# A list scheduler that repeats itself with ranks from latest start times

## The chip, the cores and the metric

The kernel runs on one core of a Trainium2 chip, as one program. The metric is device time in microseconds (us). It was timed three times; the median is 1887.29 us. One further execution was taken by the profiler, and every row shown here is from that one.

## The reference

One inference step of a layer with three kinds of head that read the same normalised input. 2048 prompt tokens and 8 x 16 sample tokens, model width 1024, all in float32.

```python
h = rms_norm(x, norm_g) @ w_in                 # 1024 -> 3654 columns
fox_cols, rwkv_cols, mem_cols = jnp.split(h, [FOX_COLS, FOX_COLS + RWKV_COLS], axis=-1)
q, k, v, logf, g_f = fox_prep(fox_cols, fox_q_g, fox_k_g, fox_b_f)
o_f = fox_prompt(q, k, v, logf)                # 6 heads x 64, causal softmax with a forget bias
xs = token_shift(rwkv_cols, shift_prev, rwkv_mu)
o_r, s_new, g_r = rwkv_branch(xs, rwkv_s0, ...)  # 6 heads x 64, S <- S diag(w) + S(-kk)^T(a kk) + v^T k
o_m = mem_attend(mq, mem_q_g, mk, mv)          # 4 heads x 64 against 256 memory tokens
o = jnp.concatenate([o_f * silu(g_f), o_r * silu(g_r), o_m * silu(g_m)], axis=-1)
y = x + o @ w_out
```

The sample tokens do the same with cached keys and values, and a state of their own for the recurrence. Outputs are y, the new keys, values and forget values, and the states.

## The kernel before

Large products are done as three matmuls of rounded parts: each operand is split into a high part (a copy rounded to the PE's fast 32-bit format) and a low part (the rest), and high x high, high x low and low x high are added. Small products stay plain float32.

**Projection phase.** Four blocks `it` of 512 tokens (the first with the 128 sample tokens). A block normalises its input (`prep_x`), and projects it in groups of 256 columns: `wd_load` brings a group's split weights (tiles `w`, four buffers in tag `hl`; the first time from the input through ACT and POOL, later from a copy `w_d` in DRAM), `proj_d` (`pjd`) or `wide` (`pjt`) multiplies. Results are copied out of PSUM (`qk`, `gth`, two buffers each) and stored to DRAM.

In each block three RWKV visits `p` of two heads each are made, twelve prompt visits in all, and three for the samples. A visit is a long chain of small steps. `rwkv_in` makes the decayed factors (`AR`, `bk`; `bk` has one buffer), multiplies them chunk by chunk (`gr` into `gm`), writes diagonal blocks to DRAM (`ld<-gm`, line 436), loads them the other way round (`yt<-ld`, line 438), inverts them on DVE in 28 small operations (`ytmp`, `yt`), writes them back (`ld<-yt`, line 447) and loads them into place (`xd<-ld`, eight transfers, line 451). `rwkv_mid` transposes `xd` (lines 464 and 477), joins the blocks with 32x32 matmuls (`gw`, `gx`), and turns factors with the PE (`pvt`, `pat`, `pbt`); the last of these reads `bk`. `rwkv_scan` carries the state through eight chunks, one after the other, and `rwkv_out` normalises and stores.

**Attention phase.** It begins where the buffers of the first phase end: its pools in SBUF and PSUM lie over those of the first. Twelve units (three head pairs x four query blocks) of forgetting attention: `pm` for row maxima, `pS` scores, `P` exponentials split into `Ph` and `Pl`, `po` values. Between them stand eight units against the memory, the sample units (`sA` to `sD`), and the output projection (`py`), in three parts.

**Order.** The kernel is first written out in program order. `_arrange` then re-sorts it. `_program` lists for each instruction an engine, a duration by a formula (`_Op`), what it depends on and which tiles it uses. `_visits` joins neighbouring small matmuls into one node. `_schedule` runs through the nodes as a simulated machine: it repeatedly takes, over all engines, the node that could start earliest. Among nodes of one engine with the same start the lowest rank wins. A tile's first user must wait for a free buffer of its tag, in program order of the tag's tiles (`pt` and `pj` may leave that order), and for the first phase's pools to be empty where its own pool lies over them. The rank is the place in program order, measured in time, less a weight times the length of the longest chain behind the node (`below`). On PE `stay` is taken off the rank of a node whose matmul shape is the one in use. Eight schedules are made (four weights, two values of `stay`), and the one with the shortest simulated total is kept. Its start times give the order on every engine, and each engine runs its instructions in that order. All transfers are issued from one queue, SP's, which runs in order too.

Of the kernel before, what the change touches and what calls it, by code (L numbers as in the profile page):

```python
# [51 lines left out]
def kernel(ctx: ExitStack, tc: tile.TileContext, I: dict, O: dict):  # L52
# [873 lines left out]
    with ExitStack() as p2:  # L926
# [523 lines left out]
_WARM = 3300  # L1450
_WINDOW = 3000
_STEP = 100
_WEIGHTS = (0.0, 0.15, 0.3, 0.45)
_STAY = (0, 2500)
_LOOSE = ("pt", "pj")


class _Pools:


    def __init__(self, tc):
        self.tc, self.open, self.below = tc, [], {}
# [236 lines left out]
        return s, s + (own - c.own) + c.time + (w - 1) * c.own  # L1699


def _schedule(prog, runs, over, weight, stay, loose=(), rank=None):

    ins, eng, cost, deps, tiles, tile = prog
    nodes, node = runs
    count = len(nodes)
    of = [eng[m[0]] for m in nodes]
    before = [sorted({node[j] for k in m for j in deps[k]} - {x}) for x, m in enumerate(nodes)]  # L1710
    used = [sorted({n for k in m for n in tiles[k]}) for m in nodes]
    seen = lambda a, b: (0 if a == "PE" else 15) if a == b != "SP" else _SEEN[b]
    succ, soft, need = [[] for _ in nodes], [[] for _ in nodes], [len(d) for d in before]
    pool = {n: t.mls.memorylocations[0].ant_tile_pool_name for n, t in tile.items()}
    first, queue, uses, left, free_at = {}, {}, {}, {}, {}
    for x in range(count):
        for j in before[x]:
            succ[j].append(x)
        for n in used[x]:
            uses[n] = uses.get(n, 0) + 1  # L1720
            left[pool[n]] = left.get(pool[n], 0) + 1
            if n not in first:
                first[n] = x
                queue.setdefault(tile[n].tag, []).append(n)
                free_at[tile[n].tag] = [0] * tile[n].tag_meta.bufs
            elif first[n] not in before[x]:
                soft[first[n]].append(x)
                need[x] += 1
    after = [sorted({q for n in used[x] for q in over.get(pool[n], ())}) for x in range(count)]
    pooled, below, at, own = {}, [0] * count, 0, [0] * count  # L1730

    def length(m, e):
        c = [cost[k] for k in m]
# [9 lines left out]
    spent = [length(m, e) for m, e in zip(nodes, of)]  # L1743
    gate = {}
    for x in range(count - 1, -1, -1):
        tail = 150 if of[x] == "PE" else 0
        below[x] = spent[x] + max([below[s] + seen(of[x], of[s]) + tail for s in succ[x]] +
                                  [gate.get(pool[n], 0) for n in used[x]], default=0)
        for q in after[x]:
            gate[q] = max(gate.get(q, 0), below[x])  # L1750
    for x in range(count):
        at += spent[x] if of[x] == "PE" else _STEP
        own[x] = at - weight * below[x]
    rank = rank or own
# [3 lines left out]
    released, alive, wire, base, order = {}, set(), 0, 0, []  # L1758
    cand = {e: [x for x in range(count) if not need[x] and of[x] == e] for e in free}

    def possible(x):
        r, taken = ready[x], {}
        for q in after[x]:
            if left.get(q):
                return None
            r = max(r, pooled.get(q, 0))
        for n in used[x]:
            if n not in alive:
                tag = tile[n].tag
                j = taken.get(tag, 0)  # L1770
                if len(free_at[tag]) <= j:
                    return None
                fresh = queue[tag][:j + 1]
                if n not in fresh:
                    if tag.rsplit("_", 2)[0] not in loose or len(free_at[tag]) <= j + 1:
                        return None
                r, taken[tag] = max(r, sorted(free_at[tag])[j]), j + 1
        return r

    while len(order) < count:  # L1780
        while done[base]:
            base += 1
        best = None
        for e, xs in cand.items():
            b = None
            for x in xs:
                r = possible(x) if x <= base + _WINDOW else None
                if r is None:
                    continue
                if e == "PE":  # L1790
                    c = cost[nodes[x][0]]
                    s, key = array.starts(c, r)
                    y = (key, rank[x] - stay * (c.shape == array.shape), x, e, s, r)
                else:
                    s = max(free[e], r)
                    y = (s, rank[x], x, e, s, r)
                if b is None or y < b:
                    b = y
            if b and (best is None or b[0] < best[0]):
                best = b  # L1800
        if not best:
            return math.inf, order, start
        _, _, x, e, s, r = best
        cand[e].remove(x)
        done[x] = True
        order.append(x)
        for n in used[x]:
# [24 lines left out]
        start[x] = s  # L1832
        gone = end[x] + 60
        for n in used[x]:
            uses[n] -= 1
            left[pool[n]] -= 1
            pooled[pool[n]] = max(pooled.get(pool[n], 0), gone)
            released[n] = max(released.get(n, 0), gone)
            if not uses[n]:
                free_at[tile[n].tag].append(released[n])  # L1840
        for z, t in [(z, s + 1) for z in soft[x]] + [(z, end[x] + seen(e, of[z])) for z in succ[x]]:
            ready[z] = max(ready[z], t if e != "PE" or of[z] != "PE" else s + 1)
            need[z] -= 1
            if not need[z]:
                cand[of[z]].append(z)
    return max(end), order, start


def _arrange(nc, tc, pools):

    prog = _program(nc)
    over, runs = _overlaps(pools, prog[-1]), _visits(prog)
# [120 lines left out]
```

## Time and profile before

| | |
|---|---|
| median of three timed runs | 1887.29 us (1883.79 to 1889.1) |
| the profiled execution, its own time | 1892.18 us |
| its span, first to last instruction | 1890.1 us |
| busy: PE, DVE, ACT, POOL | 94%, 50%, 46%, 42% |
| mean granted clock of PE | 0.954 |
| moved by the transfers | 301.34 MB, 159 GB/s on the mean |

The page cuts the span into 40 slices of 47 us. A digit is the busy share in tenths; `PEclk` is the clock granted to PE, in tenths of the full one.

```profile
PE   5979999899999999998999997899898999999998
DVE  6544444464444563453744543767445544386213
ACT  5424342424234323324232424687687555876452
PEclk9989999999999999998999896799999889999999
```

PE's low slices are the first, those near slices 24 and 25 (1130 to 1220 us), where the first phase ends, and one at slice 31 (1460 to 1500 us). The clock is low at the same places. ACT works much more in the second half, where the exponentials are.

### The profile page before, as it was taken

What the parts mean: (1) busy time and instruction counts of PE and PEld (TensorE: products, weight loads), DVE (VectorE), ACT (ScalarE), POOL (GpSimd) and SP (SyncE); (2) the same over time, 40 slices, a digit from 0 to 9 for tenths busy, and PEclk for the clock granted to TensorE, in tenths of its full rate; (3) what the DMA queues carried; (4) which work ended last, traced back from release to release, by engine and by line L of the source; (5) the groups of instructions that cost most, each with busy time, mean ns of one, the idle gap of its engine ahead of it and who ended that gap; (6) DMA issues with size and microseconds to landing.
All of it is one profiled execution on the core that took longest, in us unless ns stands there. A gap on an engine that the chain in (4) does not pass through costs nothing. (4 is left out here: it accounts for less than half of the span.)

```text
span 1890.1 us, 42104 instructions
## 1 busy us (share of the span) xinstructions
PE 1784.7 (94%) x16743; PEld 1426.4 (75%) x16743; DVE 949.0 (50%) x2330; ACT 874.9 (46%) x1727; POOL 788.9 (42%) x790
## 2 busy tenths in 40 slices
PE   5979999899999999998999997899898999999998
PEld 4878988688887888776788886666665666667776
DVE  6544444464444563453744543767445544386213
ACT  5424342424234323324232424687687555876452
POOL 5564342142132232121321331377485443866463
PEclk9989999999999999998999896799999889999999
DMA  7665455535436555354455344435546644254332
GB/s 245 228 227 169 153 175 182 191 123 176 163 117 207 177 167 196 109 176 163 127 164 188 103 155 123 141 126 167 188 137 209 186 139 137 67 179 145 137 114 100
DMA packets 213274, 301.34 MB, mean 159 GB/s; under 512 B 57444, under 2 KB 162454, under 8 KB 197206
## 3 DMA queue, kind: packets, MB, share of 16 engines
q1 hardware_dynamic: 213078, 298.66, 48.2%
q8 instruction: 131, 2.15, 0.5%
q14 instruction: 65, 0.53, 0.1%
HBM read 211.47 MB, written 87.12 MB: 158 GB/s over the span
## 5 line engine op out<-in xcount | busy, mean ns | idle before, releaser
L59 PE MATMUL pjd<-xk,w 128*128 128x512 f32 (+5 forms) x2280 | 526.4, 375 | 18.9 <-ACT qk L705 6.7
L59 PEld LDWEIGHTS pjd<-xk,w 128*128 128x128 f32 (+1 forms) x2280 | 385.8, 191 | 87.4 <-issue 9.5
L62 POOL TENSOR_TENSOR Pl<-P,Ph 128x512 fp32r<-128x512 f32 (+3 forms) x272 | 315.5, 1170 | 165.5 <-ACT Ph L1120 144.7
L59 PE MATMUL pjt<-w,xk 128*128 128x256 f32 x2040 | 290.3, 291 | 6.7 <-POOL w L62 4.2
L59 PEld LDWEIGHTS pjt<-w,xk 128*128 128x128 f32 x2040 | 266.2, 194 | 17.8 <-issue 5.0
L59 PE MATMUL py<-W,oh 128*128 128x512 f32 x816 | 247.1, 403 | 1.9 <-DVE rb L1162 0.9
L1117 ACT ACTIVATE P<-pS,NB 128x512 f32<-128x512 f32 x240 | 148.5, 623 | 110.9 <-PE pS L59 85.0
L59 PEld LDWEIGHTS py<-W,oh 128*128 128x128 f32 x816 | 150.9, 190 | 39.7 <-DVE rb L1162 1.4
L59 PE MATMUL pS<-Q,K 128*128 128x512 f32 (+2 forms) x480 | 160.1, 400 | 4.5 <-ACT P L1117 4.0
L59 PE MATMUL po<-Ph,vt 128*65 128x512 f32 x480 | 158.3, 381 | 0.3 <-ACT ob L1143 0.2
L1120 ACT CAST Ph<-P 128x512 fp32r<-128x512 f32 (+3 forms) x272 | 151.4, 564 | 9.2 <-PE po L59 4.0
L59 PEld LDWEIGHTS pS<-Q,K 128*128 128x128 f32 (+1 forms) x480 | 89.1, 198 | 36.6 <-ACT P L1117 16.0
L62 DVE TENSOR_TENSOR xo<-py,xo 128x512 f32<-128x512 f32 x68 | 46.8, 689 | 133.2 <-PE py L59 133.0
L1063 DVE CUSTOM_DVE_ANT_0 jk<-pm,nb,mx 128x512 bf16<-128x512 f32 (+3 forms) x144 | 93.0, 646 | 30.6 <-PE pm L59 22.8
L62 POOL TENSOR_TENSOR nr<-nr,mhalf 128x8 f32<-128x8 f32 (+2 forms) x43 | 61.5, 1431 | 97.5 <-DVE nr L68 73.0
L59 PE MATMUL pm<-K,Q 128*128 128x512 f32 (+2 forms) x240 | 96.4, 415 | 5.7 <-DVE mx L1063 4.8
L62 POOL TENSOR_TENSOR w<-wraw,w 128x1024 fp32r<-128x1024 f32 (+1 forms) x34 | 80.7, 2375 | 44.3 <-ACT w L197 43.2
L59 PE MATMUL po<-Pl,vt 128*65 128x512 f32 x240 | 91.1, 380 | 0.6 <-POOL Pl L62 0.6
L59 PEld LDWEIGHTS po<-Ph,vt 128*65 128x65 f32 x480 | 65.2, 141 | 26.6 <-issue 2.2
L705 ACT COPY qk<-pjt 128x512 f32<-128x512 f32 (+1 forms) x47 | 26.5, 563 | 113.1 <-PE pjt L59 92.0
L1063 DVE CUSTOM_DVE_ANT_0 jk<-pm,nb 128x512 bf16<-128x512 f32 (+3 forms) x96 | 61.3, 638 | 33.0 <-PE pm L59 28.3
L62 POOL TENSOR_TENSOR oh<-ot,oh 128x384 fp32r<-128x384 f32 (+2 forms) x38 | 45.2, 1191 | 57.0 <-ACT oh L1321 32.0
(392 smaller groups left out, 2942.6 us busy)
## 6 DMA issues: line engine op xcount, KB each, us to landing
w<-w_d SPq DMA_DIRECT2D x84, 1024.0 KB
w_d<-w SPq DMA_DIRECT2D x28, 1024.0 KB
y_d<-xo SPq DMA_DIRECT2D x21, 512.0 KB
wraw<-in_w_in SPq DMA_DIRECT2D x36, 256.0 KB
xo<-in_x SPq DMA_DIRECT2D x17, 512.0 KB
xo<-y_d SPq DMA_DIRECT2D x17, 512.0 KB
xt<-in_x SPq DMA_DIRECT2D x24, 256.0 KB
xraw<-in_xT SPq DMA_DIRECT2D x24, 256.0 KB
```

The costliest lines, as they stand in the source:

```text
L59: PE.matmul(out, lhsT, rhs, start=start, stop=stop, skip_group_check=True)
L62: e.tensor_tensor(out=out, in0=a, in1=b, op=op)
L705: S.copy(o_, out)
L1063: V.tensor_tensor_reduce(out=jk[:, :n], in0=pm[:, :n], in1=U["nb"][:, h, c0:c0 + n], scale=1.0, scalar=-3.0e38 if c0 == 0 else m_, op0=A_, ...
L1117: S.activation(P_[:, c0:], pS[:, c0:], AF.Exp, bias=NB[:, qb, 2 * hp + h, kt:kt + 1] if fox else 0.0)
L1120: S.copy(Ph[:, c0:], P_[:, c0:])
```

## The change

`_schedule` is split: what doesn't change between schedules goes into a class `_Problem` (dependencies, tiles, `below`), and the rank is handed in. `_Problem.emitted(weight)` is the old rank. While a schedule is made, it is noted for each node which earlier node's end freed the buffer or the pool that it took (`why`). At the end a pass backward over the schedule gives each node a latest start `late`: the latest at which every node that depends on it, or that waited for its buffer, can still start at its own latest. The order on the engines does not count in it. `_arrange` makes five schedules for each of three weights (0.3, 0.45, 0.6), all with `stay` 0; after each the ranks become 0.6 of the old ones plus 0.4 of `late`. The shortest of the fifteen is kept. Nothing before `_WEIGHTS` in the file changes, and the simulated machine, its durations and its rules stay.

```diff
-_WEIGHTS = (0.0, 0.15, 0.3, 0.45)
-_STAY = (0, 2500)
+_TRIES = ((0.3, 0), (0.45, 0), (0.6, 0))
+_AGAIN = 5
+_SHIFT = 0.4
...
+    def emitted(self, weight):
+
+        at, rank = 0, []
+        for x in range(self.count):
+            at += self.spent[x] if self.of[x] == "PE" else _STEP
+            rank.append(at - weight * self.below[x])
+        return rank
...
-            r = max(r, pooled.get(q, 0))
+            r = max(r, pooled.get(q, (0,))[0])
...
+        for q in p.after[x]:
+            if q in pooled:
+                why[x].append((pooled[q][1], pooled[q][0]))
         for n in used[x]:
             if n not in alive:
                 alive.add(n)
                 queue[tile[n].tag].remove(n)
                 free_at[tile[n].tag].sort()
-                free_at[tile[n].tag].pop(0)
+                at, by = free_at[tile[n].tag].pop(0)
+                if by >= 0:
+                    why[x].append((by, at))
...
-    return max(end), order, start
+    total = max(end)
+    late = [total - (end[x] - start[x]) for x in range(count)]
+    for x in reversed(order):
+        e = of[x]
+        for j in p.before[x]:
+            late[j] = min(late[j], late[x] - (1 if of[j] == e == "PE" else end[j] - start[j] + p.seen(of[j], e)))
+        for j, at in why[x]:
+            late[j] = min(late[j], late[x] - (at - start[j]))
+    return total, start, late
...
-    _, _, start = min((_schedule(prog, runs, over, w, stay, _LOOSE) for w in _WEIGHTS for stay in _STAY),
-                      key=lambda x: x[0])
+    found = []
+    for w, stay in _TRIES:
+        rank = p.emitted(w)
+        for _ in range(_AGAIN):
+            total, start, late = _schedule(p, rank, stay, _LOOSE)
+            rank = [(1 - _SHIFT) * a + _SHIFT * b for a, b in zip(rank, late)]
+            found.append((total, start))
+    _, start = min(found, key=lambda x: x[0])
```

More of the change, by code (lines that the diff above doesn't have):

```diff
@@ L1699, in run @@
         return s, s + (own - c.own) + c.time + (w - 1) * c.own
[L1702 to L1733, printed above, removed]
@@ new lines, with __init__, seen, length @@
+class _Problem:
+    def __init__(self, prog, runs, over):
+        self.ins, self.eng, self.cost, deps, tiles, self.tile = prog
+        self.nodes, node = runs
+        nodes, tile = self.nodes, self.tile
+        self.count = count = len(nodes)
+        self.of = of = [self.eng[m[0]] for m in nodes]
+        self.before = before = [sorted({node[j] for k in m for j in deps[k]} - {x}) for x, m in enumerate(nodes)]
+        self.used = used = [sorted({n for k in m for n in tiles[k]}) for m in nodes]
+        self.succ, self.soft, self.need = [[] for _ in nodes], [[] for _ in nodes], [len(d) for d in before]
+        self.pool = pool = {n: t.mls.memorylocations[0].ant_tile_pool_name for n, t in tile.items()}
+        self.queue, self.uses, self.left, first = {}, {}, {}, {}
+        for x in range(count):
+            for j in before[x]:
+                self.succ[j].append(x)
+            for n in used[x]:
+                self.uses[n] = self.uses.get(n, 0) + 1
+                self.left[pool[n]] = self.left.get(pool[n], 0) + 1
+                if n not in first:
+                    first[n] = x
+                    self.queue.setdefault(tile[n].tag, []).append(n)
+                elif first[n] not in before[x]:
+                    self.soft[first[n]].append(x)
+                    self.need[x] += 1
+        self.after = [sorted({q for n in used[x] for q in over.get(pool[n], ())}) for x in range(count)]
+        self.spent = [self.length([self.cost[k] for k in m], e) for m, e in zip(nodes, of)]
+        self.below, gate = [0] * count, {}
+        for x in range(count - 1, -1, -1):
+            tail = 150 if of[x] == "PE" else 0
+            self.below[x] = self.spent[x] + max([self.below[s] + self.seen(of[x], of[s]) + tail for s in self.succ[x]] +
+                                                [gate.get(pool[n], 0) for n in used[x]], default=0)
+            for q in self.after[x]:
+                gate[q] = max(gate.get(q, 0), self.below[x])
+    @staticmethod
+    def seen(a, b):
+        return (0 if a == "PE" else 15) if a == b != "SP" else _SEEN[b]
+    @staticmethod
+    def length(c, e):
@@ L1741, in length, with _schedule @@
         return c[0].own
[L1743 to L1754, printed above, removed]
+    def emitted(self, weight):
[4 more added lines that the diff above has]
+        return rank
+def _schedule(p, rank, stay, loose=()):
+    nodes, cost, of, used, tile, pool, count = p.nodes, p.cost, p.of, p.used, p.tile, p.pool, p.count
+    need, uses, left = list(p.need), dict(p.uses), dict(p.left)
+    queue = {t: list(q) for t, q in p.queue.items()}
+    free_at = {t: [(0, -1)] * tile[q[0]].tag_meta.bufs for t, q in queue.items()}
     free = dict.fromkeys(("PE", "DVE", "Activation", "Pool", "SP"), 0)
@@ L1757, in _schedule @@
     ready, end, done, start = [0] * count, [0] * count, [False] * count, [0] * count
-    released, alive, wire, base, order = {}, set(), 0, 0, []
+    released, alive, pooled, wire, base, order, why = {}, set(), {}, 0, 0, [], [[] for _ in nodes]
     cand = {e: [x for x in range(count) if not need[x] and of[x] == e] for e in free}
@@ L1776, in possible @@
                         return None
-                r, taken[tag] = max(r, sorted(free_at[tag])[j]), j + 1
+                r, taken[tag] = max(r, sorted(free_at[tag])[j][0]), j + 1
         return r
@@ L1801, in _schedule @@
         if not best:
-            return math.inf, order, start
+            return math.inf, start, start
         _, _, x, e, s, r = best
@@ L1806, in _schedule @@
         order.append(x)
+        for q in p.after[x]:
+            if q in pooled:
+                why[x].append((pooled[q][1], pooled[q][0]))
         for n in used[x]:
@@ L1836, in _schedule @@
             left[pool[n]] -= 1
-            pooled[pool[n]] = max(pooled.get(pool[n], 0), gone)
-            released[n] = max(released.get(n, 0), gone)
+            pooled[pool[n]] = max(pooled.get(pool[n], (0, x)), (gone, x))
+            released[n] = max(released.get(n, (0, x)), (gone, x))
             if not uses[n]:
                 free_at[tile[n].tag].append(released[n])
-        for z, t in [(z, s + 1) for z in soft[x]] + [(z, end[x] + seen(e, of[z])) for z in succ[x]]:
+        for z, t in [(z, s + 1) for z in p.soft[x]] + [(z, end[x] + p.seen(e, of[z])) for z in p.succ[x]]:
             ready[z] = max(ready[z], t if e != "PE" or of[z] != "PE" else s + 1)
@@ L1845, in _schedule @@
                 cand[of[z]].append(z)
-    return max(end), order, start
+    total = max(end)
[7 more added lines that the diff above has]
+    return total, start, late
 def _arrange(nc, tc, pools):
     prog = _program(nc)
-    over, runs = _overlaps(pools, prog[-1]), _visits(prog)
-    _, _, start = min((_schedule(prog, runs, over, w, stay, _LOOSE) for w in _WEIGHTS for stay in _STAY),
-                      key=lambda x: x[0])
+    runs = _visits(prog)
+    p = _Problem(prog, runs, _overlaps(pools, prog[-1]))
+    found = []
[6 more added lines that the diff above has]
+    _, start = min(found, key=lambda x: x[0])
     at = {}
```

1 line of the change is left out of this document (removed).

## The prediction

> **What bounds the kernel now.** I read the page first, for the busiest engine and the clock, then the windows, to place the loss by stage.
>
> ```profile
> PE 1784.7 (94%) x16743; PEld 1426.4 (75%) x16743; DVE 949.0 (50%) x2330; ACT 874.9 (46%) x1727; POOL 788.9 (42%) x790
> ...
> core 0: 1890.1 us, clock 0.954
> ```
>
> TensorE (PE) is busy 1784.7 of 1890.1 us, and no other engine passes half. Two things are lost on it: 1890.1 - 1784.7 = 105.4 us of idle time, and clock. The granted clock is 0.954 on the mean, so about 1784.7 x 0.046 = 82.1 us of the busy time is the price of the reduced clock (an estimate, which takes the mean clock for the busy time). Together 187.5 us. What is left, some 1703 us, is work that an order can't change.
>
> The windows say where it lies. Columns: from:to, length, then busy us (and instructions) of PE, PE's weight loads, DVE, ACT, POOL; clock; DMA share; GB/s.
>
> ```profile
> 0.00:50.00 50.00, 29.48 (x147) 23.52 (x148) 32.01 (x74) 28.32 (x62) 23.65 (x35) 0.93 0.81 255
> 104.00:150.00 46.00, 37.51 (x397) 35.72 (x396) 18.88 (x49) 13.45 (x23) 26.23 (x21) 0.85 0.74 243
> 1133.00:1182.00 49.00, 39.31 (x636) 31.42 (x634) 18.92 (x47) 23.19 (x48) 8.65 (x12) 0.64 0.40 118
> 1182.00:1230.00 48.00, 42.98 (x181) 28.79 (x181) 38.09 (x98) 30.55 (x61) 19.70 (x21) 0.80 0.44 139
> 1446.00:1504.00 58.00, 49.58 (x291) 34.55 (x290) 32.61 (x90) 27.55 (x57) 19.11 (x22) 0.82 0.63 192
> 1850.00:1890.10 40.10, 34.60 (x156) 25.73 (x154) 17.37 (x23) 8.67 (x17) 8.97 (x10) 1.00 0.24 89
> ```
>
> The loss of a window is its length less PE's busy time, plus busy time x (1 - clock). The head loses 20.5 + 2.1 = 22.6, waiting for the first inputs; the tail 5.5, the last additions and stores. I count both as fixed: 187.5 - 28.1 = 159.4 us can be reached by order. Of it the three stretches in between hold 68.9: the border between the projection phase and the attention phase (1133 to 1230) 23.8 + 13.6 = 37.5, the decode units (1446 on) 17.3, and 104 to 150 14.1. The remaining 90.5 is spread thinner over the other 1600 us.
>
> Why the border is bad: dense matmuls run out before the last RWKV visit's chain does.
>
> ```profile
> 1046.91 1.77 DVE L65 SCALAR_TENSOR_TENSOR e<-e,e 128x512 f32<-128x512 f32 x1
> ...
> 1069.90 2.34 DVE L65 SCALAR_TENSOR_TENSOR bk<-xsk,vh,e 128x512 f32<-128x512 f32 x1 [0.51 <-PE pbt L59]
> ...
> 1105.44 0.16 DVE L62 TENSOR_TENSOR ytmp<-yt 64x14 f32<-64x14 f32 x1
> ...
> 1109.34 0.21 DVE L62 TENSOR_TENSOR yt<-yt,ytmp 64x54 f32<-64x54 f32 x1
> 1110.40 0.69 DVE L65 SCALAR_TENSOR_TENSOR gth<-gth,pjd 128x512 f32<-128x512 f32 x1 [0.85 <-ACT gth L751]
> ...
> 1119.78 0.17 DVE L62 TENSOR_TENSOR yt<-yt,ytmp 64x14 f32<-64x14 f32 x1
> ...
> 1133.14 0.48 PE L59 MATMUL pjd<-xk,w 128*128 128x512 f32 x1
> ```
>
> These are rows of the timeline, DVE's and at the end PE's: start, length, engine, what is written from what. The last projection matmul starts at 1133.14. The visit's triangular solver (`yt`, `ytmp`) ends only at 1119.95, its result comes back from DRAM (`xd`) after 1130, and everything behind that (gw, gx, the scan, the output) runs with almost nothing dense beside it, at a clock of 0.64.
>
> **The change, part by part.** The program's instructions stay, so no count and no duration changes; what changes is the order on each engine and on SP's transfer queue. Before, the best of eight list schedules is kept (four weights, with and without a bonus for staying in a matmul shape). After, the best of fifteen: three weights without the bonus, five passes each, every next pass with ranks moved 0.4 towards the latest start that data and buffers leave in the pass before. Each pass still starts what can start earliest; the rank decides only between instructions that could start at the same time. So nothing is held back on purpose, and the gain is limited to places where something urgent stood behind something that could wait. I look for such places on the worst chain.
>
> The solver of the last visit goes from 1105.44 to 1119.95, 14.5 us. Its first 18 of 28 operations take 4.11 us to 1109.55, so 28 alone would take 4.11 / 18 x 28 = 6.4. The other 8.1 us DVE spent on instructions of gates (`gth`, at 1110.40) and norms that came between. The solver's transfers stand in SP's queue like this:
>
> ```profile
> 434.65 0.47 SPq L447 DMA_DIRECT2D ld<-yt  x1
> 436.61 3.46 SPq L451 DMA_DIRECT2D xd<-ld  x7
> ...
> 1034.72 0.46 SPq L447 DMA_DIRECT2D ld<-yt  x1
> 1040.40 0.33 SPq L192 DMA_DIRECT2D w<-w_d  x1
> 1040.82 5.04 SPq L451 DMA_DIRECT2D xd<-ld  x8
> ...
> 1120.30 0.45 SPq L447 DMA_DIRECT2D ld<-yt  x1
> ...
> 1125.79 0.46 SPq L713 DMA_DIRECT2D out_mv_p<-qk  x1
> 1126.34 3.80 SPq L451 DMA_DIRECT2D xd<-ld  x8
> ```
>
> From the write `ld<-yt` to the first `xd<-ld` an early visit needs 436.61 - 434.65 = 1.96 us; the last one 6.04 (stores of memory keys and values stand between, the last of them at 1125.79) and the one before it 6.10 (behind a weight load, `w<-w_d`). That is 4.1 us too much in each. Sum of what better ranks could take out ahead of the naked stretch: 8.1 + 4.1 + 4.1 = 16.3 us. A us less of naked chain is a us of it moved beside dense work, and the naked window (1133 to 1182) loses 23.8 / 49 = 0.49 per us. So the border yields 16.3 x 0.49 = **7.9 us**, 21% of its loss. Its bounds: 0, if these waits merely change place, and 37.5.
>
> For the other two stretches (31.4 us) I have no such count; I give them the same 21%, **6.6 us**, with 0 and 31.4 as bounds. For the thin rest I take a tenth, **9.1 us**, because a new order also makes new gaps there; its lower bound is the slower rival below, its upper one 90.5.
>
> What is moved past what: with late ranks, weight loads and the RWKV visit's transfers come ahead of result stores in SP's queue. What then becomes late are stores, and the buffers that they hold. The first row shows the kind already, the second is used below:
>
> ```profile
> PE pjd L59 <- ACT qk L705: 6.7, 2, 3.9
> ...
> PEld L59 <- issue: 24.2, 104, 0.5
> ```
>
> PE waited 6.7 us in two waits for `qk` copies, whose two buffers are free again only when their stores are through. The latest starts go through buffer releases too, so such a store gets an early date where a tile waits for its buffer. I put no net cost on it. The shape bonus goes: a change of shape shows as "issue" before weight loads, 24.2 us in 104 waits, 0.23 each, and mostly beside a busy PE. Between none and 50 changes more that is 0 to 11.5 us; I take 0, since nearly all of it is covered by the matmul before, and keep 11.5 in the range.
>
> Sum: 7.9 + 6.6 + 9.1 = 23.6 us gained. The profiled execution took 1892.2 us (span 1890.1 and 2.1 around it), 4.9 above the median of the three timed runs, 1887.29. So 1892.2 - 23.6 - 4.9 = 1863.7, **1864 us**.
>
> A rule that speaks against this: the Trainium skill, "Perfetto Trace Analysis", section "Optimization Strategy", says that a gap which repeats through a stretch can mean too few buffers for the next tile. By it the order would gain nothing at the border, and the sum would be that of the second rival below.
>
> **Rivals.**
>
> *More.* `e`, a factor of `bk`, was done at 1048.7, yet `bk` was written only at 1069.90, when PE had read out the visit before: 21.2 us. If the visit before comes earlier, these go too: (16.3 + 21.2) x 0.49 = 18.3 us at the border, 49% of its loss. The same share of the three stretches is 33.8, and 21% of the rest 19.0: 52.8 gained, 1834.5, so 1834 us. For it: the delays lie one behind the other on one chain. Against: each pass moves the ranks only by 0.4, and most of the waits are not PE's.
>
> *Nothing: buffers, not order.* `bk` has one buffer, and the 21.2 us above are a wait for it. The weight tiles have four and are handed out in program order. Then the passes find plans that differ only on paper, 1887 us. The Trainium skill's rule above is this case, and these rows agree with it for `bk`. The same time comes out if the best plan is a first pass that was in the old list too, so that the repetition does nothing.
>
> *Slower: plans too tight for the chip.* An urgent matmul is put where its operand is due on paper. If that comes later, PE stands, since its queue is served in order too, and the clock falls. The place is gw, the first matmul behind the visit's trip through DRAM:
>
> ```profile
> PEld gw L59 <- DVE x L464: 3.7, 5, 1.8
> ...
> 1050.00:1055.00 5.00, 3.37 (x140) 2.93 (x140) 2.46 (x7) 1.15 (x3) 0.00 (x0) 0.92 0.02 5
> 1055.00:1060.00 5.00, 5.00 (x65) 4.49 (x65) 0.51 (x2) 2.34 (x6) 0.00 (x0) 0.50 0.02 3
> 1060.00:1065.00 5.00, 5.00 (x100) 4.59 (x95) 0.00 (x0) 1.14 (x3) 0.00 (x0) 0.56 0.01 3
> ```
>
> One such stall left 1.63 us idle, and in these 15 us 3.37 x 0.08 + 5 x 0.50 + 5 x 0.44 = 5.0 of clock: 6.6 us. Weight loads waited there in 5 of 12 prompt visits (3.7 us). If the other 7 came to stall as hard, 46.2 us go against 23.6: 1892.2 + 22.6 - 4.9 = 1909.9, so 1910 us. It decides from 23.6 / 6.6, that is from 4 visits on.
>
> **How the numbers follow.** Forecast (1846 to 1881) 0.52; more 0.18; nothing 0.16; slower 0.14. I take 0.3% (5.7 us, so 1881.6 to 1893.0) as what a measurement can tell from no change: faster 0.70, same 0.16, slower 0.14. The range takes in the forecast, the nothing case with the 11.5 us of shape changes partly against it, more than half of "more" and the start of "slower": 1828 to 1897. About 0.07 is left out below and 0.10 above.
>
> **What would show it.** Right: as many instructions as before; PE idle near 93 us and a clock near 0.96; in the last visit, fewer stores between `ld<-yt` and `xd<-ld`, a solver nearer 6.4 than 14.5 us, and a naked stretch under 35 us. Wrong: a border of the old length with `bk` waiting some 21 us (nothing); gw and gx with many waits and clocks of 0.5 inside 100 to 1050 us (slower); windows of 5 us all full at 1.00 through the border (more). The forecast is wrong above all if the share that I carry from the border to the other windows doesn't hold there.

## The result, and the profile after

The median of four timed runs is 1835.59 us (1834.19 to 1837.16); the kernel before, run beside it, took 1888.19 (1883.79 to 1889.83). The ratio is 0.9722, with a 95% interval of 0.9707 to 0.9737: 52.6 us faster, where 24 were forecast. The profiled execution took 1835.97 us.

These are the lines of the page on PE, its rows in the 40 slices, and the row of the core with the granted clock.

```profile
PE 1745.5 (95%) x16743; PEld 1396.3 (76%) x16743; DVE 933.9 (51%) x2330; ACT 871.2 (48%) x1727; POOL 785.5 (43%) x790
...
PE   4989989999999999999999997899899999999998
...
PEclk9999999999999999999999998899899899999999
```

```profile
core 0: 1833.9 us, clock 0.975
```

The same 16743 matmuls now keep PE busy for 1745.5 us instead of 1784.7, because fewer of them run at the reduced clock: at the full one it would be some 1702 us in both (1784.7 x 0.954, 1745.5 x 0.975). Idle time is 1833.9 - 1745.5 = 88.4 us (105.4 before). The clock costs 1745.5 x 0.025 = 43.6 us (82.1 before). Together 132.0 against 187.5, so 55.5 us, which is the difference of the two spans, 56.2, within rounding. More than two thirds of it, 38.5 us, is clock.

The windows below answer those of the prediction: the head; the stretch around the end of the first visit's trip (moved by 18 us, since that trip ends 18 us later); the two halves of the border (moved by 57.7 us, by which the first phase ends sooner); the decode units (cut, as before, 4 us ahead of the dip); and the tail.

```profile
0.00:50.00 50.00, 24.48 (x108) 20.36 (x109) 31.22 (x72) 26.76 (x57) 23.50 (x33) 0.93 0.80 252
...
122.00:168.00 46.00, 42.08 (x429) 39.85 (x430) 23.72 (x67) 20.15 (x42) 24.73 (x23) 0.93 0.53 173
1075.30:1124.30 49.00, 45.09 (x717) 37.44 (x716) 13.35 (x32) 14.30 (x31) 11.56 (x13) 0.93 0.30 96
1124.30:1172.30 48.00, 31.92 (x148) 21.84 (x147) 35.22 (x83) 30.73 (x62) 12.41 (x18) 0.72 0.67 201
...
1406.00:1464.00 58.00, 54.70 (x315) 35.94 (x314) 33.38 (x99) 28.91 (x59) 21.71 (x24) 0.85 0.59 200
1793.80:1833.90 40.10, 32.88 (x147) 24.71 (x145) 17.38 (x23) 5.94 (x13) 6.47 (x9) 0.97 0.24 89
```

Loss is counted as before (length less busy, plus busy x (1 - clock)):

| stretch | before | after | gained | forecast |
|---|---|---|---|---|
| border, two windows | 37.5 | 7.1 + 25.0 = 32.1 | 5.4 | 7.9 |
| stretch at 104 (now 122) to 150 (168) | 14.1 | 6.9 | 7.2 | 6.6 with the next |
| decode units | 17.3 | 11.5 | 5.8 | |
| head and tail | 28.1 | 27.2 + 8.2 = 35.4 | -7.3 | 0 |
| all the rest | 90.5 | 46.1 | 44.4 | 9.1 |

So the border gave about what was forecast, and the "thin rest" gave five times as much. The largest single piece of it, 17.3 us, lies between the ninth and the tenth visit's `x<-xd`, where a new block begins. First the kernel before: the whole stage, then its first 30 us in steps of 10.

```profile
848.45:980.55 132.10, 123.24 (x1304) 101.64 (x1302) 75.56 (x210) 43.45 (x96) 32.91 (x38) 0.92 0.51 167
...
850.00:860.00 10.00, 8.18 (x210) 5.60 (x198) 2.51 (x5) 4.62 (x12) 1.59 (x3) 0.66 0.94 347
860.00:870.00 10.00, 7.19 (x129) 6.40 (x130) 1.25 (x3) 3.26 (x8) 0.63 (x2) 0.66 0.20 75
870.00:880.00 10.00, 8.31 (x156) 7.25 (x157) 4.04 (x9) 5.67 (x14) 2.33 (x5) 0.83 0.33 102
```

Then the kernel after, the same stage of its work.

```profile
824.78:947.06 122.28, 120.92 (x1315) 97.31 (x1314) 75.11 (x217) 45.95 (x102) 37.06 (x40) 1.00 0.54 178
...
825.00:835.00 10.00, 10.00 (x281) 7.11 (x280) 4.28 (x8) 6.04 (x14) 1.36 (x3) 1.00 0.45 140
835.00:845.00 10.00, 10.00 (x164) 7.33 (x164) 4.41 (x10) 5.79 (x14) 2.81 (x4) 1.00 0.76 283
845.00:855.00 10.00, 10.00 (x168) 8.18 (x165) 4.43 (x10) 4.62 (x10) 2.34 (x5) 1.00 0.86 254
```

Dense matmuls of these 30 us are `pjd`; the same windows for that tile alone (columns: PE, its weight loads, DVE, ACT, then clock and transfers), first before, then after:

```profile
850.00:880.00 30.00, 4.84 (x12) 1.89 (x13) 0.69 (x1) 1.16 (x2) 0.72 0.49 175
```

```profile
825.00:855.00 30.00, 17.80 (x65) 9.83 (x64) 2.07 (x3) 3.06 (x5) 1.00 0.69 226
```

Before, only 12 dense matmuls (4.84 us) lie beside the visit's small ones. PE is idle for 6.3 us of these 30, and its clock is 0.66, 0.66 and 0.83. After, 65 dense ones (17.80 us) do, PE is full and the clock 1.00. The stage's loss falls from 8.86 + 9.86 = 18.7 to 1.4 us. A further 6.4 us of the rest lie in the stage behind it, up to the last visit's `x<-xd` (6.7 us lost before, 0.3 after); the other 21 are spread over the span.

At the last visit the rows are these: DVE's, SP's and the last projection matmul, all of the kernel after.

```profile
1021.18 0.69 DVE L65 SCALAR_TENSOR_TENSOR e<-e,e 128x512 f32<-128x512 f32 x1 [0.91 <-POOL e L68]
1023.22 1.75 DVE L65 SCALAR_TENSOR_TENSOR bk<-xsk,vh,e 128x512 f32<-128x512 f32 x1
...
1048.44 0.41 DVE L62 TENSOR_TENSOR ytmp<-yt 64x14 f32<-64x14 f32 x1 [0.48 <-DMA yt<-ld]
...
1067.28 0.62 DVE L62 TENSOR_TENSOR yt<-yt,ytmp 64x14 f32<-64x14 f32 x1
```

```profile
1067.93 0.45 SPq L447 DMA_DIRECT2D ld<-yt  x1
...
1071.11 3.65 SPq L451 DMA_DIRECT2D xd<-ld  x8
```

```profile
1119.32 1.43 PE L59 MATMUL pjd<-xk,w 128*128 128x512 f32 x5
```

`bk` is written at 1023.22, 1.4 us after its factor `e` is done (1021.18 + 0.69), where it waited 21.2 us before. That holds for the last visit alone. In the eleventh, whose factor is done at 944.31, `bk` still comes 17.7 us later (16.6 before):

```profile
962.04 0.75 DVE L65 SCALAR_TENSOR_TENSOR bk<-xsk,vh,e 128x512 f32<-128x512 f32 x1 [1.57 <-PE pbt L59]
```

The last visit's solver takes longer than before: 1048.44 to 1067.28 + 0.62, 19.5 us against 14.5. From `ld<-yt` to `xd<-ld` it is 3.2 us, not 6.0. The last dense matmul ends at 1120.8. The first phase ends with the last write of `bv`:

```profile
1182.63 0.69 DVE L62 TENSOR_TENSOR bv<-bv,xsg 128x512 f32<-128x512 f32 x1
```

```profile
1124.89 0.69 DVE L62 TENSOR_TENSOR bv<-bv,xsg 128x512 f32<-128x512 f32 x1
```

That is at 1183.3 before and 1125.6 after. So the stretch without dense matmuls (last dense matmul to the end of the phase, the **naked stretch**) shrank from 49.7 to 4.8 us. What comes behind it is a new hole, shown here in windows of 5 us, with the row of PE's waits that names it.

```profile
1120.00:1125.00 5.00, 2.77 (x27) 1.84 (x25) 3.48 (x9) 1.64 (x4) 4.94 (x9) 1.00 0.57 159
1125.00:1130.00 5.00, 0.69 (x5) 0.42 (x4) 2.66 (x5) 4.50 (x10) 0.39 (x1) 0.87 1.04 244
1130.00:1135.00 5.00, 4.00 (x13) 2.79 (x13) 2.83 (x11) 1.07 (x2) 0.00 (x0) 0.50 1.03 359
```

```profile
PE pm L59 <- DVE Q L62: 12.2, 7, 4.8
```

These are the first copies of the attention phase's `Q`, before and after:

```profile
1146.56 0.69 DVE L62 TENSOR_TENSOR Q<-pt,Q 64x512 fp32r<-64x512 f32 x1 [2.16 <-ACT Q L1050]
```

```profile
1129.89 0.69 DVE L62 TENSOR_TENSOR Q<-pt,Q 64x512 fp32r<-64x512 f32 x1
```

Before, the first `Q` was there 36 us ahead of the end of the first phase, so its loads and transposes lay beside the naked stretch. After, it comes 4 us behind that end. PE waits 12.2 us for `Q` in all, and the clock falls to 0.50. Over the whole span the first phase became 57.7 us shorter and the rest 1.5 us longer:

```profile
0.00:1183.30 1183.30, 1111.38 (x13279) 949.31 (x13280) 587.14 (x1478) 424.42 (x884) 382.99 (x416) 0.95 0.51 168
1183.30:1890.10 706.80, 673.35 (x3466) 477.06 (x3464) 361.89 (x854) 450.52 (x843) 405.90 (x374) 0.96 0.44 145
```

```profile
0.00:1125.60 1125.60, 1073.75 (x13245) 920.55 (x13245) 558.75 (x1454) 413.71 (x865) 380.57 (x416) 0.99 0.53 172
1125.60:1833.90 708.30, 671.74 (x3498) 475.76 (x3498) 375.18 (x876) 457.54 (x864) 404.88 (x374) 0.96 0.46 152
```

### The profile page after: what moved, and what is told of

Read it like the earlier page. It is cut to its first block, busy times and chain, and to the rows that moved or that the text cites. A ratio compares the mean times of both kernels' runs of the same rounds, so it can differ in the third digit from the quotient of the medians.

```text
span 1833.9 us, 42044 instructions
## 1 busy us (share of the span) xinstructions
PE 1745.5 (95%) x16743; PEld 1396.3 (76%) x16743; DVE 933.9 (51%) x2330; ACT 871.2 (48%) x1727; POOL 785.5 (43%) x790
## 3 DMA queue, kind: packets, MB, share of 16 engines
q1 hardware_dynamic: 213078, 298.66, 49.7%
## 5 line engine op out<-in xcount | busy, mean ns | idle before, releaser
L59 PE MATMUL pjd<-xk,w 128*128 128x512 f32 (+4 forms) x2280 | 520.6, 373 | 12.9 <-DVE xk L62 6.3
L59 PE MATMUL py<-W,oh 128*128 128x512 f32 x816 | 239.3, 403 | 2.3 <-DVE rb L1162 1.6
L1117 ACT ACTIVATE P<-pS,NB 128x512 f32<-128x512 f32 x240 | 147.2, 622 | 93.1 <-PE pS L59 70.5
L59 PE MATMUL pS<-Q,K 128*128 128x512 f32 (+1 forms) x480 | 155.1, 391 | 4.5 <-ACT P L1117 4.3
L59 PE MATMUL po<-Ph,vt 128*65 128x512 f32 x480 | 152.9, 377 | 0.9 <-ACT ob L1143 0.7
L59 PE MATMUL pm<-K,Q 128*128 128x512 f32 (+2 forms) x240 | 95.4, 410 | 14.4 <-DVE Q L62 12.2
```

The lines of the kernel that those rows point to most:

```text
L59: PE.matmul(out, lhsT, rhs, start=start, stop=stop, skip_group_check=True)
L1117: S.activation(P_[:, c0:], pS[:, c0:], AF.Exp, bias=NB[:, qb, 2 * hp + h, kt:kt + 1] if fox else 0.0)
```

## The experiments

The fifteen schedules of the changed kernel are `found[0]` to `found[14]`: five passes for each of the weights 0.3, 0.45 and 0.6. The one kept is `found[12]`, the third pass with 0.6. **Planned** is the simulated total that the kernel's own `_schedule` computes; it was 1795.5 us for the order of the kernel before and 1773.1 for the changed one. So the plan had promised 22.4 of the 52.6 us. All ratios below are to the kernel before, measured beside each; "first phase" is the end of the last `bv` in the profiled execution, and its loss is idle time plus clock, added up over windows cut at the visits. The windows give the clock to two decimals, so these clock losses are good to some 3 us; and a profiled execution lies up to 8.3 us from the median of its kernel's runs. Only the changed kernel and combo are faster by more than 2% (some 38 us) over their whole interval; where the text calls another run faster, its interval ends below 1, but the gain is small. p30_1, ph1_2, nowhy_2 and chain_60 have two timed runs each, 13 us apart in the first two.

| run | planned | measured | ratio (95%) | first phase, rest | loss of the first phase: idle + clock |
|---|---|---|---|---|---|
| before | 1795.5 | 1888.2 | 1 | 1183, 707 | 71.9 + 50.1 |
| after | 1773.1 | 1835.6 | 0.9722 (0.9707 to 0.9737) | 1126, 708 | 51.8 + 10.3 |
| p60_0 | 1802.5 | 1891.1 | 0.998 (0.9957 to 1.0003) | 1183, 707 | 71.8 + 44.9 |
| p30_1 | 1778.7 | 1861.5 | 0.9832 (0.9737 to 0.9928) | 1142, 725 | 55.6 + 19.6 |
| p45_2 | 1786.9 | 1875.4 | 0.9907 (0.9864 to 0.9951) | 1150, 724 | 67.8 + 19.0 |
| p60_3 | 1814.3 | 1878.8 | 0.9929 (0.9899 to 0.9959) | 1155, 721 | 78.2 + 21.7 |
| nowhy_2 | 1964.2 | 2030.5 | 1.0762 (1.0676 to 1.0848) | 1244, 780 | 137.2 + 63.8 |
| ph1_2 | 1784.1 | 1857.8 | 0.9847 (0.9754 to 0.994) | 1122, 728 | 52.9 + 6.3 |
| sp_2 | 1801.2 | 1897.2 | 1.0044 (1.0022 to 1.0065) | 1192, 704 | 83.7 + 35.4 |
| nosp_2 | 1772.3 | 1875.6 | 0.9927 (0.9897 to 0.9957) | 1141, 724 | 62.4 + 16.5 |
| bk1_45 | 1797.7 | 1875.6 | 0.9932 (0.9917 to 0.9947) | 1169, 709 | 64.1 + 40.3 |
| bk2_45 | 1790.1 | 1885.3 | 0.997 (0.9949 to 0.9991) | 1185, 706 | 77.4 + 40.0 |
| pe_4 | 1780.6 | 1874.2 | 0.9928 (0.9898 to 0.9958) | 1154, 720 | 73.3 + 27.5 |
| nope_4 | 1781.9 | 1880.2 | 0.9947 (0.9919 to 0.9974) | 1154, 725 | 68.0 + 15.8 |
| chain_60 | 1787.6 | 1860.7 | 0.9863 (0.9814 to 0.9913) | 1143, 717 | 60.0 + 18.4 |
| last1 | 1782.8 | 1887.3 | 0.9984 (0.9961 to 1.0006) | 1159, 733 | 70.1 + 28.3 |
| combo | 1764.1 | 1845.7 | 0.9755 (0.9716 to 0.9793) | 1137, 709 | 59.8 + 15.7 |

### Other passes of the same search

Is it the repetition, or only that more orders were tried? Four other schedules of the fifteen were run, the first of them without any repetition.

```diff
-    _, start = min(found, key=lambda x: x[0])
+    _, start = found[10]
```

p30_1, p45_2 and p60_3 take `found[1]`, `found[7]` and `found[13]`.

> Weight 0.6, first pass: no repetition. Its simulated total is 1802.5 us; that of the order before is 1795.5 (chip 1888.2, so 92.7 more), that of the changed one 1773.1 (chip 1835.6, so 62.5 more). Theory A, the chip follows the plan and the rest of the difference scatters from order to order by some 15 us whatever the ranks: 1802.5 + 77 = 1880 (1865 to 1895). Theory B, orders made from latest starts lose less on the chip than orders made from program order: 1802.5 + 92 = 1895 (1885 to 1905).

> Weight 0.3, second pass: ranks moved once. Simulated total 1778.7 us. Theory A: 1778.7 + 77 = 1856 (1841 to 1871). Theory B: 1778.7 + 62 = 1841 (1831 to 1851), if one step of 0.4 is enough for the effect.

> Weight 0.45, third pass: the order before, repeated twice. Simulated total 1786.9 us, 8.6 less than the first pass of the same weight, which is the order before. Theory A: 1786.9 + 77 = 1864 (1849 to 1879). Theory B: 1786.9 + 62 = 1849 (1839 to 1859).

> Weight 0.6, fourth pass: one pass behind the order that was kept, with a simulated total of 1814.3 us, 41 longer than that and 19 longer than the order before. Theory A: 1814.3 + 77 = 1891 (1876 to 1906), no faster than before. Theory B: 1814.3 + 62 = 1876 (1866 to 1886), faster than before although its plan is longer.

The order without repetition (p60_0) is no faster than before, and its first phase is as long. All three repeated orders are faster, although p60_3 has the longest plan of the four. In each the first phase is 29 to 42 us shorter, and its clock costs 19 to 22 us in place of 45 to 50. But the rest is 14 to 18 us longer, which the kept order avoids. So these three gain 13 to 32 us (the ratios times 1888); 52.6 is the best of the four repeated orders. A gain of 13 alone would not show that repetition does it: bk1_45 below, a first pass, is 12.6 us faster than the kernel before. What sets the repeated orders apart in the traces is the naked stretch. It is 49.7 us before, 54.0 in p60_0 and 49.5 in bk1_45, but 5.1 in p30_1, and in p45_2 and p60_3 the last dense matmul ends as late as the phase does. With that stretch closed the four repeated orders still lie 43 us apart, so closing it is not what the 52.6 us are.

The second theory, that repeated orders always lose some 30 us less than first passes, falls with p30_1 and p45_2. The first theory's ranges, 30 us wide, hold in all four runs, though p60_3 was faster than before and was not to be. By it the changed kernel would have taken 1850 us; it is 14.5 us below that.

### Parts of the rule

In nowhy_2 the latest starts no longer go through buffers and pools:

```diff
-        for j, at in why[x]:
-            late[j] = min(late[j], late[x] - (at - start[j]))
...
+    _, start = found[12]
```

In ph1_2, sp_2 and nosp_2 the ranks are moved only for nodes ahead of the attention phase (`x < two`), only on SP's queue, and everywhere but there; with `found[12]`, `found[12]` and `found[7]`.

```diff
-            rank = [(1 - _SHIFT) * a + _SHIFT * b for a, b in zip(rank, late)]
+            rank = [(1 - _SHIFT) * a + _SHIFT * b if e == 'SP' else a for x, (a, b, e) in enumerate(zip(rank, late, p.of))]
```

> The changed kernel's own pass (weight 0.6, third), but the latest starts are taken from data alone: the lines that carry them back through freed buffers and pools are left out. Simulated total 1964.2 us. If the buffers are what makes the latest starts useful: about 1964 + 75 = 2040 (2000 to 2080), far slower than before. If the data chains alone carry the gain and the planner only misjudges it: below 1880.

> The same pass with the ranks moved in the projection phase alone; the attention phase keeps program-order ranks. Simulated total 1784.1 us, the first phase ending at 1088.8 (changed kernel 1773.1 and 1088.4). If the gain is the first phase's: it ends at 1126 to 1145 instead of 1183, and with 708 to 725 for the second the span is 1834 to 1870. If the second phase's ranks carry part of it: above 1870.

> The same pass with the ranks moved on SP's transfer queue alone. Simulated total 1801.2 us, the first phase ending at 1128.0. The prediction counted 8.2 of the 16.3 us on the last chain in this queue: then about 1880, the first phase some 4 us shorter. If the queue's order isn't what limits the chain: 1885 to 1900, the first phase ending at 1183 or later.

> Ranks moved on all engines but the transfer queue; weight 0.45, third pass, the best of its fifteen plans: simulated total 1772.3 us, the first phase ending at 1086.9. If the engines' ranks carry the gain: 1832 to 1860, the first phase ending at 1125 to 1145. If the queue's ranks are needed: above 1870.

Without the buffer releases this pass does harm (7.6%). Its plan was bad too (1964.2), and the other fourteen passes of that search were not run. The queue's ranks alone bring nothing (0.4% slower). Everything but the queue brings 0.7%, with a plan 0.8 us better than that of the changed kernel: 40 us apart on the chip, and 0.8 the other way on paper. The first phase of nosp_2, 1141 us, ended where the theory that the engines' ranks carry the gain had it; its time, 1875.6, fits the other theory, that the queue's are needed. With the ranks moved in the first phase only, that phase is as short as in the changed kernel, but the rest isn't:

```profile
1122.10:1849.70 727.60, 681.36 (x3499) 482.14 (x3498) 375.00 (x876) 462.35 (x862) 402.61 (x374) 0.94 0.45 148
```

727.6 against 708.3 us, so some 20 us of the gain come from the repetition's effect on the second phase. In the changed kernel too that phase begins with the hole, and its order makes up for it further back.

### One buffer or two

The rival "buffers, not order" asks for a second buffer of `bk`. The room for it comes from raw inputs (`xraw`, two buffers instead of three) and from `ya`, which shares the buffer of `za`; bk1_45 is the control, which gives up the same room and keeps one `bk`. Both are the kernel before with the one weight and `stay` that won there.

```diff
-            bk = rv.tile([128, 8, 2, 64], F32, tag="bk", name="bk")
+            bk = rv.tile([128, 8, 2, 64], F32, tag="bk", name="bk", bufs=2)
...
-            ya = rv.tile([128, 8, 64], F32, tag="ya", name="ya")
+            ya = rv.tile([128, 8, 64], F32, tag="za", name="ya")
...
-_WEIGHTS = (0.0, 0.15, 0.3, 0.45)
-_STAY = (0, 2500)
+_WEIGHTS = (0.45,)
+_STAY = (0,)
```

> Control for the run with two bk buffers: the old planner with its winning setting alone (weight 0.45, no bonus), with one bk buffer, but with the same room taken from raw inputs (xraw 2 instead of 3) and ya in za's buffer. The planner's own total is 1797.7 us against 1795.5 for the kernel before. Both theories: 1875 to 1905 us, first phase 1175 to 1195 us with a clock loss near 45, like the kernel before; if the room taken matters by itself, it is seen here.

> As the control, but bk has two buffers, so that the 21 us wait of bk for the visit before is not there. Planned total 1790.1, 7.6 below the control. Theory buffers: the one buffer held the last visits back, and any order without that wait gets most of the gain; the time is 25 to 50 us below the control, and the first phase ends before 1155 us with a clock loss under 25. Theory order: the wait was only one effect of small matmuls being ranked behind dense ones; bk is written early, but the matmuls that read it come no sooner, the time is within 15 us of the control, and the clock loss of the first phase stays above 35.

These are the last visit's rows with two buffers: DVE's, and PE's last dense matmul.

```profile
1048.94 1.78 DVE L65 SCALAR_TENSOR_TENSOR e<-e,e 128x512 f32<-128x512 f32 x1
1052.51 0.74 DVE L65 SCALAR_TENSOR_TENSOR bk<-xsk,vh,e 128x512 f32<-128x512 f32 x1
```

```profile
1131.51 0.48 PE L59 MATMUL pjd<-xk,w 128*128 128x512 f32 x1
```

The wait is gone (1048.94 + 1.78 to 1052.51, 1.8 us; in the eleventh visit also 1.8), and the time is 9.7 us above the control, not 25 to 50 below it; the naked stretch is still 52.8 us (1132.0 to 1184.8). Taking the 21.2 us away by a buffer brings nothing under the old planner; two buffers under the new one were not run. The control has its own lesson: it is 12.6 us faster than the kernel before with a plan 2.2 us longer. So much the chip can differ from the plan without a reason that the plan shows.

### A head start by hand

In chain_60 nothing is repeated. One pass with weight 0.6 gets 60 us off the rank of every node that uses a visit's tiles; in last1 (weight 0.45, 30 us) only those of the last visit.

```diff
+    chain = [any(p.pool[n] in ('pg', 'ps', 'rv') or p.tile[n].tag.rsplit("_", 2)[0] in ('yt', 'ytmp', 'AD') or n[:2] in ('AR', 'WX', 'XT', 'yt')
+                 for n in p.used[x]) for x in range(p.count)]
+    rank = [a - 60000 * c for a, c in zip(p.emitted(0.6), chain)]
+    _, start, _ = _schedule(p, rank, 0, _LOOSE)
```

In last1, with `cut` 60 nodes ahead of the last `bk`:

```diff
+    rank = [a - 30000 * (c and x >= cut) for x, (a, c) in enumerate(zip(p.emitted(0.45), chain))]
```

> No repetition: one pass with weight 0.6 in which every node of an RWKV visit (its small tiles and PSUM tiles) gets its rank lowered by 60 us. Planned total 1787.6, first phase 1103.2. Theory head start: it is enough that the visits run ahead, however that comes about; first phase 1125 to 1155 us, clock loss under 25, time 1840 to 1880 us. Theory latest starts: which instructions are urgent must come from the plan's own slack; a blanket head start takes as much from the dense work as it gives, first phase over 1165 us, time 1880 to 1910 us.

> The old planner's best setting (weight 0.45, no bonus), one pass, with the rank of the last prompt visit's nodes alone lowered by 30 us. Planned total 1782.8, against 1795.5 for the kernel before. Theory last visit: the loss is the end of the phase without dense matmuls; as soon as the last visit starts sooner, the stretch after the last dense matmul shrinks from 50 us to under 25 and the time is 1845 to 1868 us. Theory all visits: the visits come one after the other, and the last can't come much sooner alone; the stretch stays over 35 us and the time is 1870 to 1895 us.

The rows of chain_60: DVE's at the last visit, and the window of the stage between the ninth and the tenth visit.

```profile
1024.22 0.69 DVE L65 SCALAR_TENSOR_TENSOR e<-e,e 128x512 f32<-128x512 f32 x1 [0.92 <-POOL e L68]
1043.06 0.88 DVE L65 SCALAR_TENSOR_TENSOR bk<-xsk,vh,e 128x512 f32<-128x512 f32 x1 [0.53 <-PE pbt L59]
```

```profile
834.00:959.00 125.00, 123.72 (x1335) 98.74 (x1335) 77.08 (x217) 46.37 (x103) 36.72 (x40) 1.00 0.55 176
```

`bk` still waits 18.1 us (1024.91 to 1043.06), yet half of the gain is there (1.4%), and the stage between the ninth and the tenth visit runs at 1.00 with 1.3 us idle. So a head start of all visits is enough for half of the gain, and the end of the wait for `bk` is no part of that half. The theory "latest starts" falls in its strict form.

The rows of last1: its last dense matmul, and windows of the same stage, of the first 40 us of the second phase, and of the whole second phase.

```profile
1149.04 0.48 PE L59 MATMUL pjd<-xk,w 128*128 128x512 f32 x1
```

```profile
848.45:980.55 132.10, 122.24 (x1305) 100.94 (x1304) 76.81 (x212) 43.70 (x98) 32.88 (x38) 0.94 0.52 167
1158.80:1198.80 40.00, 27.90 (x126) 19.15 (x127) 30.05 (x71) 25.33 (x51) 9.95 (x14) 0.66 0.60 193
1158.80:1891.90 733.10, 687.85 (x3498) 486.04 (x3498) 376.66 (x875) 458.69 (x860) 403.53 (x375) 0.93 0.45 145
```

With a head start of the last visit alone the naked stretch shrinks from 49.7 to 9.3 us (1149.5 to 1158.8), and the first phase by 24.5. The time stays the same (0.9984, to 1.0006). The second phase takes 733.1 us instead of 706.8. Of the 26.3 more, 11.8 are idle time (733.10 - 687.85 against 706.80 - 673.35) and the rest busy time at a lower clock, 0.93 for 0.96. Its first 40 us lose 12.1 + 27.90 x 0.34 = 21.6 us, where the kernel before loses 12.7:

```profile
1183.30:1223.30 40.00, 34.98 (x148) 23.16 (x147) 31.89 (x80) 24.29 (x49) 16.32 (x18) 0.78 0.46 143
```

The other part is lost further back, the largest piece of it from 1519 to 1639 us, where 19.9 us are lost and 9.6 in the like window of the kernel before. The stage between the visits is as bad as before (0.94). Each theory was half wrong: the last visit can come sooner alone, and that is worth nothing, since the second phase takes it all back.

### Which engine, and both together

pe_4 moves ranks on PE only, nope_4 everywhere but on PE (weight 0.6, fifth pass, their planned best); combo takes a head start of 30 us for the visits (weight 0.45) and four passes from there. The diffs are pe_4's and combo's.

```diff
-            rank = [(1 - _SHIFT) * a + _SHIFT * b for a, b in zip(rank, late)]
+            rank = [(1 - _SHIFT) * a + _SHIFT * b if e == 'PE' else a for a, b, e in zip(rank, late, p.of)]
```

```diff
+    rank = [a - 30000 * c for a, c in zip(p.emitted(0.45), chain)]
+    for _ in range(4):
+        _, start, late = _schedule(p, rank, 0, _LOOSE)
+        rank = [(1 - _SHIFT) * a + _SHIFT * b for a, b in zip(rank, late)]
```

> Ranks moved towards the latest starts on PE alone, the other engines and the transfer queue keep the old rank; weight 0.6, fifth pass, planned total 1780.6 (first phase 1106.0). Theory order on PE: what counts is that PE takes the visits' small matmuls ahead of dense ones; 1845 to 1875 us, first phase 1125 to 1155 us, clock loss of it under 25. Theory all engines together: DVE and ACT must serve the chain too; 1875 to 1895 us, first phase over 1165 us, clock loss over 35.

> Ranks moved towards the latest starts on DVE, ACT, POOL and the transfer queue, PE keeps the old rank (weight 0.6, fifth pass). Planned total 1781.9, first phase 1092.7; the mirror image, PE alone, was planned at 1780.6 and took 1874. Theory PE: without PE's ranks the visits' matmuls still stand behind dense ones; over 1880 us and a stretch after the last dense matmul over 40 us. Theory any engine: each engine that serves the chain earlier brings part of the gain; 1850 to 1880 us, and that stretch under 25 us.

> Head start and repetition together: weight 0.45, the visits' ranks lowered by 30 us, then four passes with ranks moved towards the latest starts; the fourth is taken. Planned total 1764.1, 9.0 below the changed kernel's 1773.1. If the two add up: 1815 to 1832 us, below the changed kernel's 1836. If both do the same thing, and the chip is 62 to 96 us above the plan as in all runs so far: 1830 to 1860 us.

PE's ranks bring 0.7%, all the others 0.5%. Each shortens the first phase by 29 to 30 us and lengthens the second by 13 to 18. Neither engine group carries the gain alone. The naked stretch closes by either group, to 6.7 us (pe_4) and 12.9 (nope_4), as the theory "any engine" had it; nope_4's time, 1880.2, lies at the edge between the two theories. The two ways of getting ahead don't add up: combo has the best plan of all, 1764.1, and takes 1845.7 us. By the ratios that is 6 us above the changed kernel, and the intervals overlap, so it can't be told from it. No version was measured faster.

## Why the prediction was half right

**The bound was right.** PE's idle time and its clock are what moved, and the work between stayed. The page counts the same 16743, 2330, 1727 and 790 instructions on the four engines. That the loss follows from dense matmuls running out beside a visit's chain was right too, and shows at the stage at 848 us as well as at the border.

**The step that failed is the size of the thin rest.** "For the thin rest I take a tenth", 9.1 us. It gave 44.4 of 90.5. The whole sum was 31.9 us too low (23.6 against 55.5); this term alone was 35.3 too low, and the errors of the others, -2.5, 6.4 and -7.3, nearly cancel. I had looked at three stretches of low slices and treated the rest as spread evenly. It was not: 18.7 us lay in one stage, 848 to 980, with the same sign as the border, small matmuls alone at a clock of 0.66. A table by stage of idle time and clock, cut at the visits, would have shown it. The bound that I gave for this term, up to 90.5, did hold it.

**The border's sum came out near, by a working that didn't happen.** Forecast 7.9, measured 5.4. The solver was to shrink from 14.5 towards 6.4 us and grew to 19.5. The 8.1 us between were misread as well, as time spent on gates and norms: for 3.9 of them DVE stood idle ahead of such instructions, waiting for ACT, and two of the solver's own operations took 2.32 and 0.54 us where their like took 0.20. Of the 4.1 us in each of two trips through the queue the last visit's gave 2.8 (6.0 to 3.2) and the one before it 2.7 (6.1 to 3.4). The naked stretch was to come down to under 35 us and came to 4.8. The border's first window gained 23.8 - 7.1 = 16.7 us by that, and its second lost 25.0 - 13.6 = 11.4 of it again, in the hole. So the near hit is luck. last1 shows the exchange alone: the naked stretch nearly gone, the time the same. The step "a us less of naked chain is a us of it moved beside dense work" left out what the naked stretch had been covering, the start of the attention phase.

**Transfers in SP's queue** were named as the first thing that ranks mend. sp_2 shows that ranks on that queue alone mend nothing.

**The other two stretches** gave 13.0 us against 6.6 forecast; head and tail, counted as fixed, cost 7.3 more.

**The rivals.** *More* named 1834, and the time is 1835.6. Its row came true in the last visit, where `bk` no longer waits, and not in the eleventh. Its reason was wrong, so that the number is luck: with two buffers the wait also goes, without gain, and chain_60 has half of the gain with the wait still there. What it named as its sign, windows of 5 us all full through the border, did not come either (0.69 of 5.00 from 1125 on). *Nothing: buffers* fell with the result, and for `bk` with the pair of runs too; the weight tiles' four buffers were not varied. The Trainium skill's rule, "Perfetto Trace Analysis", section "Optimization Strategy", that a repeating gap can mean too few buffers, doesn't hold here for `bk`: bk2_45 has the buffer and is 9.7 us above its control. The rows that spoke for it showed a wait ahead of a DVE instruction, not a gap that repeats on PE. The same section says that a kernel with regimes between which the most contended engine changes may gain from interleaving them. The stage at 848 is near to that, though PE is the busiest engine in its rows before and after: with 12 dense matmuls among them the small ones had a clock of 0.66 to 0.83, with 65 of 1.00.

*Slower: plans too tight* did not come. The row for it is gw's:

```profile
PEld gw L59 <- DVE x L464: 3.4, 5, 1.3
```

3.4 us in 5 waits, against 3.7 in 5 before. The other seven visits did not come to stall. The shape bonus, put at 0 in the sum, needs no price: the row "issue" before weight loads, 24.2 us in 104 waits before, is 22.0 in 97 after.

**What the 52.6 us are made of.** 22.4 were in the plan. The other 30.2 are the distance from plan to chip, 92.7 us before and 62.5 after. Over the 17 orders measured that distance runs from 62.5 to 104.5, and the changed kernel's is the smallest of all. At the middle one (88.5) its plan would have given 1861.6, so some 26 us are, as far as these runs show, the luck of this order. nosp_2, with the same plan to 0.8 us, is 40 us slower. In the profiled executions the first phase of the changed kernel ends 37.2 us behind its plan (1125.6, planned 1088.4), that of nosp_2 54.4 (1141.3, planned 1086.9). No run tells which property of an order makes that distance small. That stays open.

## What to carry to other kernels

When an order is changed, cut the trace into stages of the work and list idle time and clock loss for each, instead of looking at the worst slices alone; a chain that runs naked can cost idle time and clock at every place where it does (here 18.7 us in a stage whose three slices of PE read 8, 9 and 9), and closing the last place alone can move the cost to what comes behind it. Take such a planner's totals as a guide to some 20 us in 1800 only (62.5 to 104.5 us from plan to chip here), and measure several of its orders: of three plans within 9 us here, 1764.1, 1772.3 and 1773.1, the chip made 1845.7, 1875.6 and 1835.6. Before a second buffer is spent on a wait, ask whether what reads it would come sooner; for `bk` it did not.

## What was not expected of the hardware

The clock is lost in steps. In the windows of 10 us above it stands at 1.00, 0.83 or 0.66; at half clock that is (1 - 0.83) x 10 / 0.5 = 3.4 us and 6.8 us of it. The stretches at 0.50 in the traces, 23 with 176.1 us together before and 13 with 93.1 after, are multiples of 3.4 us, all but the last of each, which runs past the last instruction. And the loss isn't in proportion to the gap: the idle 1.63 us in the prediction's windows from 1050 on were followed by a window with PE busy for all 5.00 us and the clock at 0.50.

A gap isn't even needed. Five of the 13 stretches after, and three of the 23 before, follow 3.4 us in which PE is busy throughout. Here is one of these, with the matmuls that fill nearly all of the 3.4 us:

```profile
1429.08 4.15 PE L59 MATMUL po<-sD,sA 128*64 128x16 f32 x64
```

```profile
1429.05:1432.46 3.41, 3.41 (x61) 3.41 (x59) 2.52 (x9) 0.92 (x2) 0.00 (x0) 1.00 0.90 297
1432.46:1435.87 3.41, 3.41 (x18) 2.49 (x16) 0.28 (x1) 0.00 (x0) 0.00 (x0) 0.50 0.48 129
```

These matmuls are 16 columns wide, and the dense ones behind them run at half clock. So a busy PE in a row is no sign of a full clock. The kernel's own simulated machine goes by how much of the array the matmuls of a tick of 3.4 us fill (`_Array`), which fits; no run here varies it. The Trainium skill, "TensorE: Matmul & The Clock Gate", section "What's actually happening", has windows of about 3.4 us, which agrees, and a clock that falls after an idle one; here 1.63 us of idle time came before the one drop, and none before the other.
